# Spreading the sample group's decays through DRAM, and taking the output gates one tile early, in a fused RWKV-7 / HGRN2 step

## The chip, the cores and the metric

The kernel runs on one core of a Trainium2 chip. The core has a matrix engine (TensorE, "PE" in the profile, with its weight loads as "PEld"), three elementwise engines (VectorE "DVE", ScalarE "ACT", GpSimd "POOL"), a sequencer that issues transfers (SyncE "SP"), and 16 DMA engines that carry them. Each engine works through its own instructions in the order of the program and waits on semaphores where an instruction needs another engine's result. The metric is the device time of one execution in microseconds. The kernel before was run three times: 1065.17 us is the median, 1065.13 and 1065.8 the ends.

## What is computed

One inference step of a decoder layer for two groups of rows: 256 prompt tokens of one new sequence, and 8 sequences ("samples") with 8 new tokens each. Both are 320 columns of the same products. Cut to what matters here:

```python
h = rms_norm(x, norm_g)
p = h @ w_in                      # one projection, 2048 x 12416
# branch A: RWKV-7, 16 heads of 64
decay = exp(-exp(w_log))
for t in tokens:                  # per sample and head, from the state s handed in
    sa = s @ kk[t]
    s  = s * decay[t] - outer(sa, kk[t] * a[t]) + outer(v[t], k[t])
    y[t] = s @ r[t]
y_a = (group_norm(y) + bonus) * silu(p_za)
# branch B: HGRN2 linear recurrence, times its own gate -> y_b
merged = sigmoid(p_ga) * (y_a @ proj_a) + sigmoid(p_gb) * (y_b @ proj_b)
y = x + merged @ w_out            # then a final rms_norm
```

Returned are the two groups' outputs and the new states. The change concerns two places: the factor by which a sample's old RWKV state `s` is multiplied over its 8 tokens (one number for each sample, head and key), and the gates `sigmoid(p_ga)` and `sigmoid(p_gb)`.

## The kernel before

**Precision by parts.** A float32 weight tile of 1024 x 128 is fetched (`raw`, 512 KB), cast by ACT to a rounded part `whi`, and DVE forms the rest `wlo = raw - whi`. Each product is then three matmuls: `whi` with the high part of the data, `whi` with its low part, `wlo` with its high part. Three buffers of each of `raw`, `whi` and `wlo` turn in a ring; one block of 8 x 3 = 24 matmuls over 320 columns uses one of them.

**Four stages.** A start (norm, transposes, the first blocks); a recorded stage, in which the projection runs beside both recurrences; the gate stage (the loop at L1622); and the output product with the final norm.

**The recorded stage.** `record_all` (L1530) records every operation of every engine, the class `Recorder` (L79) then lists them in the order of a planned schedule: it walks through time with a cost for each operation and a latency for each dependency, and picks by longest remaining path. All of it is emitted at L199, so rows of the profile there are told apart by tile names. The projection's matmuls write the tile `mps`, small products write `bank` (six PSUM banks, lent in turn). DMAs are issued on SP in the planned order. A DMA that goes through a DRAM scratch tile is planned with 4500 ns from issue to data.

**A head pair.** `rwkv(p, ...)` (L916) handles two heads of 64, for p = 0 to 7 ("first" to "eighth pair"). Rows of a tile are 2 heads x 64 keys or values. `B` is the running sum of the log decays, and `f` (L955) holds their exponentials: columns 0 to 7 for the prompt's four chunks, columns 8 to 15 the whole decay of each of the 8 samples, with the key on the partition. The old sample states `s0` have the head and value on the partition, and sample and key along the row, so `f` has to be turned and repeated over 64 values. `samples()` does that by products (L1211 to L1227): POOL copies `f` into `fh` and `fq`, DVE forms the low parts in `fq`, POOL multiplies `fq` by an identity pattern to get `fd` (128 x 256, twice), PE multiplies `fd` by a block of ones (`jr_sum`) into a bank, and DVE multiplies `s0` by that bank. Later DVE adds the new outer products (tile `big`, PE output) to `s0`, and SP stores it.

A different round trip through DRAM, in every pair: `nd` (buffer name `big`) and `dns` go to scratch tiles `scr` and `scrs`, and come back into `ww` as small triangular blocks that DVE inverts step by step (rows `big<-ww`, `ww<-ww,big`). All such transfers and the weight fetches share SP's queue.

**The gate stage.** For each of 16 tiles m of 128 output columns: the gate `ga` is fetched from DRAM where it was made in the recorded stage (m < 7) or made here (48 matmuls into `mps`, then three ACT operations in `sigm`), the gate `gbt` is made here, then 24 matmuls into `ppa` (`y_a` by `proj_a`), 24 into `ppb`, and DVE and ACT merge them. Ahead of the loop `split` (L1611) divides `ya` and `yb` into high and low parts `yah`, `yal`, `ybh`, `ybl`: four ACT casts and four DVE subtractions each.

Of the kernel before, what the change touches and what calls it, by code (L numbers as in the profile page):

```python
# [9 lines left out]
F32 = mybir.dt.float32  # L10
F32R = mybir.dt.float32r
# [8 lines left out]
NT = NP_ + NS  # L20
NSEQ = 8
LS = 8
KT = D // 128
# [404 lines left out]
def hybrid_step(ctx, tc, x_prompt, x_sample, state_rwkv, state_hgrn, state_shift, norm_g, w_in,  # L428
# [4 lines left out]
    V, S, G, T = nc.vector, nc.scalar, nc.gpsimd, nc.tensor  # L433

    S.add_instruction(mybir.InstLoadActFuncSet(
        name=nc.get_next_instruction_name(), act_func_set_id=EXP_LN_SET, ins=[], outs=[]))
# [30 lines left out]
    HS = [slice(0, 64), slice(64, 128)]  # L467
# [29 lines left out]
    def run(gen):  # L497
        for _ in gen:
            pass
# [3 lines left out]
    def main(c0, post, pre=()):  # L503
        ps = psm.tile([128, 512], F32, name="mps", tag="m")
        yield from project(ps[:, :NT], win, c0, KT, hhi, hlo, pre)
        post(ps[:, :NT])


    with tc.tile_pool(name="start", bufs=1) as st, \
# [63 lines left out]
        id32 = ctile([128, 32], "id32")  # L573
# [245 lines left out]
    def sigm(out, in_, bias=0.0, sign=1.0):  # L819

        S.activation(out, in_, AF.Exp, scale=-sign, bias=bias)
        S.activation(out, out, AF.Ln, bias=1.0)
        S.activation(out, out, AF.Exp, scale=-1.0)
# [36 lines left out]
             "w1": 384, "w2": 320, "w3": 320, "ks": 128, "rhs2": 128, "ye": 192, "ket": 256, "o": NT}  # L860


    CLEAR = {"uB", "uE", "ys", "dn", "rhs", "rhs2", "k3", "vm", "w1", "vt", "att", "attc", "az", "rz"}

    def at(name, shape=(128, NT), tag=None, bufs=1, dt=F32):
        tag = tag or name
        return ring(pa, tag, list(shape), bufs, dt, SIZES.get(tag), tag in CLEAR)

# [4 lines left out]
    def aps(name="aps"):  # L873
        book.loans += 1
        at_ = lent[0]
        return bass.AP(at_.tensor, at_.offset + book.loans * LOAN, [list(d_) for d_ in at_.ap])
# [39 lines left out]
    def rwkv(p, r, k, v, za):  # L916
# [9 lines left out]
        s0 = at("s0", (128, NSEQ, 64))  # L926
# [10 lines left out]
        s = at("s", tag="uS")  # L937
# [4 lines left out]
        a = at("a", tag="uA")  # L942
# [9 lines left out]
        B = at("B", tag="uB")  # L952
        V.tensor_tensor_scan(B, rs_a, s, 0.0, op0=ALU.mult, op1=ALU.add)
        e = at("e", (128, 16))
        f = at("f", (128, 16), bufs=2)  # L955
        V.tensor_copy(e[:, 0:4], B[:, 31:NP_:64])
        Bp = B[:, :NP_].rearrange("p (c t) -> p c t", t=64)
        V.tensor_sub(Bp, Bp, e[:, 0:4, None].to_broadcast([128, 4, 64]))
# [7 lines left out]
        S.activation(e2, B, AF.Exp, scale=C0)  # L966
        S.activation(f[:, 0:4], e[:, 0:4], AF.Exp, scale=C0)
        S.activation(f[:, 4:16], e[:, 4:16], AF.Exp, scale=-C0)

        uv = at("uv", (128, 5, 2, 64))  # L970
        G.memset(uv[0:64, 0:5:2], 0.0)
# [48 lines left out]
        az = at("az", (128, 2, 2, 96))  # L1020
# [50 lines left out]
        for i in range(1, 7):  # L1071
            m = 7 - i
# [128 lines left out]
        def samples():  # L1201
            rhs = at("rhs2", (128, 64))
            S.copy(rhs, psr[:, :64])
            yield
            pu = aps("pu2")
            T.matmul(pu[:, :64], ys.rearrange("p h t -> p (h t)"), rhs, start=True, stop=True)
            for h in range(2):
                S.copy(uv[0:64, 4, h], pu[HS[h], 0:64])


            fh = at("fh", (128, 8), dt=F32R)  # L1211
            fq = at("fq", (128, 2, 8), dt=F32R)
            G.tensor_copy(fh, f[:, 8:16])
            for h in range(2):
                for hf in range(2):
                    src, dst = (slice(64 * h + 32 * j, 64 * h + 32 * j + 32) for j in (hf, 0))
                    G.tensor_copy(fq[dst, hf], f[src, 8:16])
                    dst = slice(64 * h + 32, 64 * h + 64)
                    V.tensor_sub(fq[dst, hf], f[src, 8:16], fh[src].bitcast(F32))
            pf = aps("pf")  # L1220
            for hf in range(2):
                fd = at("fd", (128, NSEQ, 32), dt=F32R)
                G.tensor_mul(fd, id32[:, None, :].to_broadcast([128, NSEQ, 32]),
                             fq[:, hf, :, None].bitcast(F32).to_broadcast([128, NSEQ, 32]))
                T.matmul(pf[:, 256 * hf:256 * hf + 256], jr_sum, fd.rearrange("p s k -> p (s k)"), start=True, stop=True)
            V.tensor_mul(s0.rearrange("p s (a k) -> p a s k", a=2), s0.rearrange("p s (a k) -> p a s k", a=2),
                         pf.rearrange("p (a s k) -> p a s k", a=2, s=NSEQ))  # L1227
            yield

            uh = at("uh", (128, 128), tag="rhs2")  # L1230
            for a_ in range(2):
                S.copy(uh[64 * a_ + 32:64 * a_ + 64], uv[64 + 32 * a_:96 + 32 * a_, 4].rearrange("p h v -> p (h v)"))
            for a_ in range(2):
                S.copy(uh[64 * a_:64 * a_ + 32], uv[32 * a_:32 * a_ + 32, 4].rearrange("p h v -> p (h v)"))
            bm = at("bm", (128, 4, 128), tag="big")
            for si in range(4):
                S.activation(bm[:, si], bk[:, 4], AF.Copy, scale=seq4[:, si:si + 1])
            pds = [aps("pd2") for _ in HS]
            side_by_side([((pds[a_][HS[h], :256], uh[HS[a_], 64 * h:64 * h + 64], bm[HS[a_], :, 64 * h:64 * h + 64]),
                           dict(start=True, stop=True)) for h in range(2) for a_ in range(2)])  # L1240
            for a_ in range(2):
                s0h = s0[:, 4 * a_:4 * a_ + 4]
                V.tensor_add(s0h, s0h, pds[a_][:, :256].rearrange("p (s k) -> p s k", s=4))
            Y.dma_start(s_rwkv[0, :, 2 * p:2 * p + 2].rearrange("s h v k -> (h v) s k"), s0)
            yield
# [243 lines left out]
    prompt_ = [scr.tile([512, 32], F32, name=f"scr{j}", tag=f"scr{j}") for j in range(2)]  # L1489
    turned = scr.tile([960, 128], F32, name="scrt", tag="scrt")  # L1490
    turned_i = scr.tile([NT, 128], F32, name="scri", tag="scri")
    pieces = lambda t_: t_.rearrange("(b x) (q c) -> q x b c", x=32, q=4)
    quads = [slice(32 * q_, 32 * q_ + 32) for q_ in range(4)]
    sample_ = [scr.tile([128, 8], F32, name=f"scrs{j}", tag=f"scrs{j}") for j in range(2)]
# [124 lines left out]

    yah, yal = split(ya, "ya", fpr, "yah")  # L1620
    ybh, ybl = split(yb, "yb", ypool, "ya")
    for m in range(KT):  # L1622
        ga = fpr.tile([128, NT], F32, name="ga", tag="ga", bufs=2)
        if m < NLATE:
            nc.sync.dma_start(ga, late[m])
        else:
            run(main(OFF_GA + 128 * m, lambda ps: sigm(ga, ps)))
        gbt = fpr.tile([128, NT], F32, name="gbt", tag="gbt", bufs=2)
        run(main(OFF_GB + 128 * m, lambda ps: sigm(gbt, ps)))
        ps = psf.tile([128, 512], F32, name="ppa", tag="f")  # L1630
        run(project(ps[:, :NT], proj_a[0], 128 * m, 8, yah, yal))
        mt = fpr.tile([128, NT], F32, name="mt", tag="mt", bufs=2)
        V.tensor_mul(mt, ga, ps[:, :NT])
        ps = psf.tile([128, 512], F32, name="ppb", tag="f")
        run(project(ps[:, :NT], proj_b[0], 128 * m, 8, ybh, ybl))
        V.tensor_mul(gbt, gbt, ps[:, :NT])
        V.tensor_add(mt, mt, gbt)
        S.copy(mhi[:, m, :], mt[:, :NP_])
        V.tensor_sub(mlo[:, m, :], mt[:, :NP_], mhi[:, m, :].bitcast(F32))
        S.copy(ms[:, m, 0], mt[:, NP_:])  # L1640
        V.tensor_sub(ms[:, m, 1], mt[:, NP_:], ms[:, m, 0].bitcast(F32))
# [168 lines left out]
```

## Time and profile before

| | before |
|---|---|
| median of 3 runs | 1065.17 us |
| the profiled execution's own time | 1065.99 us |
| its span, first to last instruction | 1063.8 us |
| granted TensorE clock, mean | 0.997 |
| DMA engines, mean rate | 168 GB/s |

The profiled execution is 0.82 us above the median, and 2.2 us of its time lie outside the span. Busy times of the engines overlap. A matmul's own duration (some 310 ns for 320 columns) also overlaps that of its neighbours; what a matmul costs PE is the step from its start to the next start, which is 0.147 us between two matmuls of 320 columns. A number in square brackets behind a row is the idle time of that engine just before it, and what ended it.

### The profile page before, as it was taken

To read this page: it belongs to the slowest core of one execution; us is meant where nothing else is said; L and a number is where in the kernel's file an instruction comes from. 1 tells how busy PE (TensorE), PEld (TensorE's weight loads), DVE (VectorE), ACT (ScalarE), POOL (GpSimd) and SP (SyncE) were. 2 spreads that over 40 slices of the span, in tenths; PEclk is the share of its full clock that TensorE was granted. 3 is DMA by queue.
4 is the path that set the end of the run, shared out by engine and by line. 5 is a ranking of instruction groups with operands and counts; after the bars stand their busy time and mean duration, and the time that the engine had idled before them with its cause. 6 is when DMAs were issued, how large, how long until landed. Compare 5 with 4: busy or idle time off the path is not lost.

```text
span 1063.8 us, 23012 instructions
## 1 busy us (share of the span) xinstructions
PE 1045.8 (98%) x8740; PEld 1010.4 (95%) x8740; DVE 763.5 (72%) x1616; ACT 697.9 (66%) x1608; POOL 127.8 (12%) x361
## 2 busy tenths in 40 slices
PE   7999999999999999999999999999999999999996
PEld 6999999999999999999999999999999999988885
DVE  8789989999999898998988857444444444446532
ACT  7757878978879689788687787444444444445412
POOL 9511201212112013112011000000000000000000
PEclk9999999999999999999999999999999999999998
DMA  6776585684865856849757647555555555497402
GB/s 202 198 184 163 126 228 142 162 224 121 216 165 123 223 147 171 210 115 214 184 139 194 175 115 219 170 165 148 156 145 152 152 146 155 144 296 266 152 17 99
DMA packets 356370, 178.78 MB, mean 168 GB/s; under 512 B 82013, under 2 KB 345440, under 8 KB 355684
## 3 DMA queue, kind: packets, MB, share of 16 engines
q1 hardware_dynamic: 355892, 176.01, 60.4%
q8 instruction: 68, 1.11, 0.4%
q10 hardware_dynamic: 368, 1.31, 0.3%
q14 instruction: 42, 0.34, 0.1%
HBM read 159.97 MB, written 17.32 MB: 167 GB/s over the span
## 4 chain that ended last, share of the span: by engine, by line
PE 94%; POOL 2%; ACT 1%; DVE 1%; DMA 1%; issue 0%; DVEq 0%; ACTq 0%; POOLq 0%
PE mps L199 47%; PE bank L199 10%; PE mps L494 5%; PE mps L493 5%; PE mps L492 5%; PE po L1682 3%; PE po L1681 3%; PE po L1683 3%; PE ppb L493 2%; PE ppb L494 2%; PE ppb L492 2%; PE ppa L494 2%; PE ppa L493 2%; PE ppa L492 2%; PE po L1687 1%; PE po L1686 1%
## 5 line engine op out<-in xcount | busy, mean ns | idle before, releaser
L199 PE MATMUL mps<-hhi,whi 128*128 128x320 f32 x1136 | 356.7, 314 | 0.0
L199 PE MATMUL mps<-hlo,whi 128*128 128x320 f32 x1136 | 355.7, 313 | 0.0
L199 PE MATMUL mps<-hhi,wlo 128*128 128x320 f32 x1136 | 354.7, 312 | 0.0
L199 PEld LDWEIGHTS mps<-hhi,whi 128*128 128x128 f32 x1136 | 213.6, 188 | 3.2 <-issue 2.3
L199 PEld LDWEIGHTS mps<-hlo,whi 128*128 128x128 f32 x1136 | 213.7, 188 | 1.2 <-issue 0.4
L199 PEld LDWEIGHTS mps<-hhi,wlo 128*128 128x128 f32 x1136 | 213.6, 188 | 1.1 <-issue 0.4
L199 DVE TENSOR_TENSOR wlo<-raw,whi 128x1024 fp32r<-128x1024 f32 x140 | 171.4, 1224 | 23.2 <-ACT whi L199 21.7
L482 ACT CAST whi<-raw 128x1024 fp32r<-128x1024 f32 x82 | 86.0, 1048 | 148.5 <-PE mps L493 93.7
L483 DVE TENSOR_TENSOR wlo<-raw,whi 128x1024 fp32r<-128x1024 f32 x82 | 100.4, 1225 | 113.3 <-ACT whi L482 113.1
L199 ACT CAST whi<-raw 128x1024 fp32r<-128x1024 f32 x140 | 146.2, 1044 | 44.0 <-PE mps L199 34.1
L493 PE MATMUL mps<-hlo,whi 128*128 128x320 f32 x400 | 123.6, 309 | 0.0
L494 PE MATMUL mps<-hhi,wlo 128*128 128x320 f32 x400 | 123.6, 309 | 0.0
L492 PE MATMUL mps<-hhi,whi 128*128 128x320 f32 x400 | 123.6, 309 | 0.0
L492 PEld LDWEIGHTS mps<-hhi,whi 128*128 128x128 f32 x400 | 75.1, 188 | 0.0
L493 PEld LDWEIGHTS mps<-hlo,whi 128*128 128x128 f32 x400 | 75.1, 188 | 0.0
L494 PEld LDWEIGHTS mps<-hhi,wlo 128*128 128x128 f32 x400 | 75.1, 188 | 0.0
L1670 DVE TENSOR_TENSOR wlo<-raw,whi 128x1024 fp32r<-128x1024 f32 x32 | 38.6, 1222 | 36.7 <-ACT whi L1669 36.5
L1669 ACT CAST whi<-raw 128x1024 fp32r<-128x1024 f32 x32 | 33.1, 1051 | 47.6 <-PE po L1686 21.7
L1681 PE MATMUL po<-whi,mhi 128*128 128x512 f32 x128 | 50.0, 391 | 0.0
L1683 PE MATMUL po<-wlo,mhi 128*128 128x512 f32 x128 | 50.0, 391 | 0.0
L1682 PE MATMUL po<-whi,mlo 128*128 128x512 f32 x128 | 50.0, 391 | 0.0
L493 PE MATMUL ppb<-ybl,whi 128*128 128x320 f32 x128 | 39.7, 310 | 0.4 <-DVE ybl L1617 0.4
(415 smaller groups left out, 1986.3 us busy)
## 6 DMA issues: line engine op xcount, KB each, us to landing
raw<-in_w_in_dram SPq DMA_DIRECT2D x194, 512.0 KB
raw<-in_w_out_dram SPq DMA_DIRECT2D x32, 512.0 KB
raw<-in_proj_a_dram SPq DMA_DIRECT2D x16, 512.0 KB
raw<-in_proj_b_dram SPq DMA_DIRECT2D x16, 512.0 KB
s<-in_state_hgrn_dram SPq DMA_DIRECT2D x8, 512.0 KB
ww<-scr SPq DMA_DIRECT2D x8, 512.0 KB
out_dram<-s SPq DMA_DIRECT2D x8, 512.0 KB
scrt<-ww SPq DMA_DIRECT2D x32, 120.0 KB
```

The costliest lines, as they stand in the source:

```text
L199: o.fn(*(real(x) for x in o.args), **{k: real(x) for k, x in o.kw.items()})
L482: S.copy(hi[:, ks], raw[:, ks])
L483: sub.tensor_sub(lo[:, ks], raw[:, ks], hi[:, ks].bitcast(F32))
L492: T.matmul(dst, hi[:, q, :], xhi[:, k, :], start=(k == 0), stop=False)
L493: T.matmul(dst, hi[:, q, :], xlo[:, k, :], start=False, stop=False)
L494: T.matmul(dst, lo[:, q, :], xhi[:, k, :], start=False, stop=(k == nk - 1))
L1669: S.copy(hi, raw)
L1670: V.tensor_sub(lo, raw, hi.bitcast(F32))
L1681: T.matmul(pt, h, hi, start=first, stop=False)
L1682: T.matmul(pt, l, hi, start=False, stop=False)
L1683: T.matmul(pt, h, lo, start=False, stop=end)
L1686: T.matmul(pt, h, hi, start=first, stop=False)
```

## The change

Two edits.

**The decays.** `f` becomes 32 columns wide and is cleared once. Right after `f` is written, DVE transposes it in blocks of 32 x 32 into `ft`. Four DMAs on SP write the sample rows of `ft` to a DRAM tile `decays` (named `scrf` in the profile), as [2 heads x 8 samples, 64 keys], and two DMAs read it back into a tile `spread`, each repeating 512 numbers over 64 partitions. The products are gone: `fh`, `fq`, `fd` and the bank. DVE multiplies `s0` by `spread`.

**The gates.** What makes `ga` and `gbt` of tile m becomes a function, and the loop calls it for tile m + 1 ahead of tile m's products with `proj_a` and `proj_b`, with three buffers of each gate for two.

```diff
-    CLEAR = {"uB", "uE", "ys", "dn", "rhs", ...}
+    CLEAR = {"uB", "uE", "ys", "dn", "f", "rhs", ...}
@@ rwkv
-        f = at("f", (128, 16), bufs=2)
+        f = at("f", (128, 32), bufs=2)
...
+        ft = at("ft", (128, 32))
+        V.transpose(ft, f)
+        for q_ in range(4):
+            Y.dma_start(decays[8 * (q_ // 2):8 * (q_ // 2) + 8, 32 * (q_ % 2):32 * (q_ % 2) + 32], ft[32 * q_ + 8:32 * q_ + 16])
+        spread = at("spread", (128, NSEQ, 64))
+        for h in range(2):
+            Y.dma_start(spread[HS[h]].rearrange("p s k -> p (s k)"),
+                        decays[8 * h:8 * h + 8].rearrange("s k -> (s k)")[None].to_broadcast([64, 512]))
@@ samples
-            fh = at("fh", (128, 8), dt=F32R)
-            fq = at("fq", (128, 2, 8), dt=F32R)
-            G.tensor_copy(fh, f[:, 8:16])
-            for h in range(2):
-                for hf in range(2):
-                    src, dst = (slice(64 * h + 32 * j, 64 * h + 32 * j + 32) for j in (hf, 0))
-                    G.tensor_copy(fq[dst, hf], f[src, 8:16])
-                    dst = slice(64 * h + 32, 64 * h + 64)
-                    V.tensor_sub(fq[dst, hf], f[src, 8:16], fh[src].bitcast(F32))
-            pf = aps("pf")
-            for hf in range(2):
-                fd = at("fd", (128, NSEQ, 32), dt=F32R)
-                G.tensor_mul(fd, id32[:, None, :].to_broadcast([128, NSEQ, 32]),
-                             fq[:, hf, :, None].bitcast(F32).to_broadcast([128, NSEQ, 32]))
-                T.matmul(pf[:, 256 * hf:256 * hf + 256], jr_sum, fd.rearrange("p s k -> p (s k)"), start=True, stop=True)
-            V.tensor_mul(s0.rearrange("p s (a k) -> p a s k", a=2), s0.rearrange("p s (a k) -> p a s k", a=2),
-                         pf.rearrange("p (a s k) -> p a s k", a=2, s=NSEQ))
+            V.tensor_mul(s0, s0, spread)
@@ gate stage
-    for m in range(KT):
-        ga = fpr.tile([128, NT], F32, name="ga", tag="ga", bufs=2)
+    def gates(m):
+        ga = fpr.tile([128, NT], F32, name="ga", tag="ga", bufs=3)
         if m < NLATE:
             nc.sync.dma_start(ga, late[m])
         else:
             run(main(OFF_GA + 128 * m, lambda ps: sigm(ga, ps)))
-        gbt = fpr.tile([128, NT], F32, name="gbt", tag="gbt", bufs=2)
+        gbt = fpr.tile([128, NT], F32, name="gbt", tag="gbt", bufs=3)
         run(main(OFF_GB + 128 * m, lambda ps: sigm(gbt, ps)))
+        return ga, gbt
+
+    made = [gates(0)]
+    for m in range(KT):
+        if m + 1 < KT:
+            made.append(gates(m + 1))
+        ga, gbt = made[m]
         ps = psf.tile([128, 512], F32, name="ppa", tag="f")
```

The schedule of the recorded stage is planned anew from these operations, so its order shifts on every engine. The first place is SP in the third pair, where the samples' decays now leave and come back beside the round trip of the triangular blocks. Before:

```order
L199 DMA out_dram<-ks_544 128x128
L199 DMA raw<-in_w_in_dram 128x8x128
L199 DMA scr_476<-big_526 32x4x32 x4
L199 DMA scrs_480<-dns_527 64x2x8
L199 DMA uv_518<-scrt 64x3x128
L199 DMA uv_518<-scrt 64x2x128
L199 DMA raw<-in_w_in_dram 128x8x128
L199 DMA w2a_0_506<-in_rwkv_a_dram 64x128
L199 DMA ww<-scr_476 128x1x1024
L199 DMA ww<-scrs_480 16x8x8
```

And with the change:

```order
L199 DMA scrf<-ft_519 8x32 x4
L199 DMA raw<-in_w_in_dram 128x8x128
L199 DMA scr_476<-big_529 32x4x32 x4
L199 DMA scrs_481<-dns_530 64x2x8
L199 DMA s_0_510<-in_state_rwkv_dram 128x8x64
L199 DMA uv_521<-scrt 64x3x128
L199 DMA uv_521<-scrt 64x2x128
L199 DMA spread_520<-scrf 64x512 x2
L199 DMA raw<-in_w_in_dram 128x8x128
L199 DMA out_dram<-s_0_535 128x8x128
L199 DMA ww<-scr_476 128x1x1024
L199 DMA ww<-scrs_481 16x8x8
```

The two reads into `spread` stand ahead of one weight fetch and of the read into `ww`. The second place is DVE in the same pair, where the inversion begins (`big<-ww`). Before (`q` and `yb` are of branch B, `ya` is branch A's result):

```order
L199 TENSOR_TENSOR fq_550<-f_515,fh_549 32x8
L199 SCALAR_TENSOR_TENSOR o_541<-o_541,cols,w_0_535 128x320
L199 TENSOR_TENSOR q_500<-q_500,w_0_533 128x320
L199 TENSOR_TENSOR yb<-o_541,w_0_539 128x320
L199 TENSOR_TENSOR wlo<-raw,whi 128x1024
L199 TENSOR_TENSOR ya<-bk_522,sg_557 128x320
L199 TENSOR_TENSOR big_526<-ww 128x30
```

And with the change:

```order
L199 TENSOR_TENSOR wlo<-raw,whi 128x1024
L199 SCALAR_TENSOR_TENSOR o_544<-o_544,cols,w_0_538 128x320
L199 TENSOR_TENSOR q_501<-q_501,w_0_536 128x320
L199 TENSOR_TENSOR yb<-o_544,w_0_542 128x320
L199 TENSOR_TENSOR ya<-bk_525,sg_558 128x320
L199 TENSOR_TENSOR rl_513<-bon_524,rh_512 128x320
L199 TENSOR_TENSOR s_0_510<-s_0_510,spread_520 128x512
L199 TENSOR_TENSOR wlo<-raw,whi 128x1024
L199 TENSOR_TENSOR big_529<-ww 128x30
```

The small `fq` row is gone, and the product of `s0` (here `s_0`) with `spread` stands just ahead of a split of weights (`wlo<-raw,whi`) and of the inversion. The third place is DVE where the gate stage begins. Before:

```order
L483 TENSOR_TENSOR wlo<-raw,whi 128x1024 x3
L1617 TENSOR_TENSOR yal<-ya,yah 128x640 x4
L483 TENSOR_TENSOR wlo<-raw,whi 128x1024
L1617 TENSOR_TENSOR ybl<-yb,ybh 128x640 x4
L1633 TENSOR_TENSOR mt<-ga,ppa 128x320
```

And with the change:

```order
L483 TENSOR_TENSOR wlo<-raw,whi 128x1024 x4
L1611 TENSOR_TENSOR yal<-ya,yah 128x640 x4
L483 TENSOR_TENSOR wlo<-raw,whi 128x1024
L1611 TENSOR_TENSOR ybl<-yb,ybh 128x640 x4
L483 TENSOR_TENSOR wlo<-raw,whi 128x1024 x2
L1634 TENSOR_TENSOR mt<-ga,ppa 128x320
```

The four splits ahead of `yal` now belong to the gates of tiles 0 and 1 (before: the gate of tile 0, then `proj_a` and `proj_b`). On PE 96 matmuls of the two gates stand ahead of the first `ppa` row, where 48 stood before, and behind that row the order is 24 into `ppa`, 24 into `ppb`, then the gate matmuls of the tile after next.

More of the change, by code (lines that the diff above doesn't have):

```diff
@@ L860, in hybrid_step @@
              "w1": 384, "w2": 320, "w3": 320, "ks": 128, "rhs2": 128, "ye": 192, "ket": 256, "o": NT}
-    CLEAR = {"uB", "uE", "ys", "dn", "rhs", "rhs2", "k3", "vm", "w1", "vt", "att", "attc", "az", "rz"}
+    CLEAR = {"uB", "uE", "ys", "dn", "f", "rhs", "rhs2", "k3", "vm", "w1", "vt", "att", "attc", "az", "rz"}
     def at(name, shape=(128, NT), tag=None, bufs=1, dt=F32):
@@ L1491, in hybrid_step @@
     turned_i = scr.tile([NT, 128], F32, name="scri", tag="scri")
+    decays = scr.tile([16, 64], F32, name="scrf", tag="scrf")
     pieces = lambda t_: t_.rearrange("(b x) (q c) -> q x b c", x=32, q=4)
```

## The prediction

> **What bounds the kernel now.** The page comes first: busy times with their shares of the span, and the chain that ended last by engine.
>
> ```profile
> PE 1045.8 (98%) x8740; PEld 1010.4 (95%) x8740; DVE 763.5 (72%) x1616; ACT 697.9 (66%) x1608; POOL 127.8 (12%) x361
> PE 94%; POOL 2%; ACT 1%; DVE 1%; DMA 1%; issue 0%; DVEq 0%; ACTq 0%; POOLq 0%
> ```
>
> PE is busy for 98% of the span and is 94% of the chain, so a change is worth what it takes off PE's instructions and what it takes out of PE's idle time. The second view, the windows by stage (stretch, length, then PE, PEld, DVE, ACT and POOL busy with counts, clock, DMA share, GB/s), says where that idle time is.
>
> ```profile
> 38.00:640.00 602.00, 600.17 (x5973) 587.62 (x5972) 534.14 (x1298) 485.75 (x1270) 96.68 (x283) 1.00 0.66 170
> 640.00:670.00 30.00, 29.30 (x199) 28.77 (x197) 19.76 (x25) 20.22 (x36) 0.00 (x0) 1.00 0.76 218
> 670.00:1045.00 375.00, 375.00 (x2299) 356.14 (x2298) 173.12 (x210) 158.19 (x232) 0.00 (x0) 1.00 0.53 161
> ```
>
> The recorded stage has 1.8 us of idle PE, the passage into the gate stage 0.7 us, the rest of the gate stage and the output product none; what stands before and behind these windows is not touched. So the second edit can gain only at the passage, and the first only its products and at most those 1.8 us with what hangs on them. The third view, PE's waits (total, times, longest), names the owners:
>
> ```profile
> PE bank L199 <- POOL fd L199: 1.5, 3, 0.6
> PE ppb L493 <- DVE ybl L1617: 0.4, 1, 0.4
> PE ppa L493 <- DVE yal L1617: 0.3, 1, 0.3
> ```
>
> Most of the idle time belongs to `fd`, which goes, and to the split of `ya` and `yb`, which gets more time. All three lines are things that the change is aimed at.
>
> **The change part by part: the products.** The group of `fd` products (durations shortest/median/longest, first and last start) and one of them in order of time:
>
> ```profile
> L199 PE MATMUL bank<-fd,jr_sum x16: 277/278/387, 66.6 to 578.7; 128*128 128x256 f32 x16
> 140.26 0.28 PE L199 MATMUL bank<-fd,jr_sum 128*128 128x256 f32 x1
> 140.38 0.30 PE L199 MATMUL mps<-hhi,whi 128*128 128x320 f32 x1
> ```
>
> A product costs PE the step to the next start, 140.38 - 140.26 = 0.12 us. Sixteen of them: **-1.9 us**. Three of the sixteen also came late:
>
> ```profile
> 349.82 0.31 PE L199 MATMUL mps<-hhi,wlo 128*128 128x320 f32 x1
> 350.56 0.38 PE L199 MATMUL bank<-fd,jr_sum 128*128 128x256 f32 x1 [0.43 <-POOL fd L199]
> 350.79 0.31 PE L199 MATMUL mps<-hhi,whi 128*128 128x320 f32 x1
> ...
> 426.50 0.31 PE L199 MATMUL mps<-hhi,wlo 128*128 128x320 f32 x1
> 427.21 0.39 PE L199 MATMUL bank<-fd,jr_sum 128*128 128x256 f32 x1 [0.40 <-POOL fd L199]
> ...
> 575.89 0.31 PE L199 MATMUL mps<-hlo,whi 128*128 128x320 f32 x1
> 576.83 0.39 PE L199 MATMUL bank<-fd,jr_sum 128*128 128x256 f32 x1 [0.64 <-POOL fd L199]
> ```
>
> The steps into them are 0.74, 0.71 and 0.94 us in place of 0.15, so 0.59 + 0.56 + 0.79 = 1.94; the step out of the first is 0.23 for 0.12, and with 0.11 for each the stalls are worth **-2.3 us**. What is late next there? Of the 1.83 us of idle PE in the recorded stage `fd` owns 1.5, which leaves 0.3 for all other causes: no second one stands right behind it.
>
> **The passage.** PE's rows where the first `ppa` and the first `ppb` products wait for the split:
>
> ```profile
> 654.98 0.31 PE L492 MATMUL ppa<-yah,whi 128*128 128x320 f32 x1
> 655.63 0.41 PE L493 MATMUL ppa<-yal,whi 128*128 128x320 f32 x1 [0.34 <-DVE yal L1617]
> 655.89 0.30 PE L494 MATMUL ppa<-yah,wlo 128*128 128x320 f32 x1
> ...
> 659.25 0.31 PE L492 MATMUL mps<-hhi,whi 128*128 128x320 f32 x1
> 659.92 0.41 PE L493 MATMUL ppb<-ybl,whi 128*128 128x320 f32 x1 [0.36 <-DVE ybl L1617]
> 660.18 0.31 PE L494 MATMUL ppb<-ybh,wlo 128*128 128x320 f32 x1
> ```
>
> Steps of 0.65, 0.26, 0.67 and 0.26 us for 0.15 each: 1.24 us. The change puts the 48 matmuls of the second gate, 48 x 0.147 = 7 us, ahead of the first `ppa` row, and the order on DVE leaves four weight splits ahead of `yal` as before. The lateness of 0.5 us is covered many times over: **-1.2 us**. Past the passage PE is 375.00 of 375.00 busy and its instructions are the same, only moved: nothing.
>
> **What is added to PE's order.** Counted from the order, the number of matmuls drops by just the 16. Two things shift. The products of `big`, in 64 x 64 tiles of the array, stand alone between 128 x 128 products in all eight pairs; before, two of the eight stood behind another tiled group and shared its switch. The small full-array product `bank<-st,arp` follows an `mps` product 18 times, before 23.
>
> ```profile
> 254.40 0.31 PE L199 MATMUL mps<-hhi,wlo 128*128 128x320 f32 x1
> 254.64 0.66 PE L199 MATMUL bank<-big,rhs 64*64 64x256 f32 x8
> 255.23 0.42 PE L199 MATMUL mps<-hhi,whi 128*128 128x320 f32 x1
> 255.49 0.22 PE L199 MATMUL bank<-st,arp 128*128 128x64 f32 x1
> ```
>
> The step into `big` is 0.24 for 0.15, and the group that stood ahead of it now has an exit of its own, for which I allow as much again: two times 0.2, **+0.4 us** (bounds 0.2 and 0.7). The step from `mps` to `st,arp` is 0.26 for 0.15; five fewer are 0.55 us, of which I take half, since the small product now has another neighbour to pay for: **-0.3 us** (bounds -0.6 and 0).
>
> **What is added beside PE.** DVE, by its groups (mean ns behind the busy time):
>
> ```profile
> L199 DVE TENSOR_TENSOR fq<-f,fh 32x8 fp32r<-32x8 f32 x32 | 5.1, 160 | 0.9
> L199 DVE STREAM_TRANSPOSE ww<-bk 128x640 f32<-128x640 f32 x8 | 6.7, 838 | 0.1
> L199 DVE STREAM_TRANSPOSE ww<-v 128x320 f32<-128x320 f32 x8 | 4.0, 500 | 0.2
> L199 DVE TENSOR_TENSOR s<-s,bank 128x512 f32<-128x512 f32 x24 | 16.4, 685 | 0.8 <-PE bank L199 0.3
> L1732 DVE TENSOR_TENSOR xa<-xa,xb 128x512 f32<-128x512 f32 x6 | 4.0, 684 | 1.3 <-ACT jk L1702 1.3
> ```
>
> 32 rows of `fq` leave (5.1 us). A transpose of 32 columns is some 0.5 - 288 x 0.338/320 = 0.2 us, eight of them 1.6 us. Multiplying `s0` costs 685 ns with a bank and should cost as much with `spread` (684 ns with both inputs in SBUF). DVE gets 3.5 us lighter over 600, and POOL, 12% busy, loses its copies and `fd`; neither bounds, so nothing is counted for it. The four clears of `f` on POOL run in its idle time.
>
> SP gets 48 DMAs, six in each pair. What matters is not their issue but two new waits: the reads into `spread` wait on SP for the writes to land, with a weight fetch, a store and the read into `ww` queued behind; and DVE's `s0` by `spread` waits for the reads, with `wlo` splits behind, for which PE waits. The nearest rows are the other round trip:
>
> ```profile
> 495.36 0.63 SPq L199 DMA_DIRECT2D ww<-scrs  x1
> 502.97 0.19 DVE L199 TENSOR_TENSOR big<-ww 128x30 f32<-128x30 f32 x1 [3.74 <-DMA ww<-scrs]
> 495.00:515.00 20.00, 20.00 (x140) 19.96 (x140) 15.34 (x38) 11.50 (x21) 1.73 (x4) 1.00 0.92 231
> SPq L199 <- DMA scrs<-ww: 7.5, 7, 1.7
> ```
>
> That read took 7.6 us from issue to data, DVE stood for 3.74 us, and PE was busy for 20.00 of the 20.00 us around it. On SP the existing pair of write and read made it wait for 1.7 us at most, and PE for nothing. In four pairs (first, third, seventh, eighth) the order leaves the time of two weight blocks, 2 x 24 x 0.147 = 7.1 us, between the earliest issue of `spread` and its use; in the other four far more. So DVE should wait for up to a microsecond or so in four pairs, well inside the 3.74 us that cost nothing. Bounds: 0; and four stalls as long as the `fd` ones, 4 x 0.7 = 2.8. Near the covered row I take **+0.4 us**.
>
> [...]
>
> **The sum.** -1.9 - 2.3 - 1.2 + 0.4 - 0.3 + 0.4 = -4.9 us. Against the profiled execution's own 1065.99 us that is 1061.1; this execution lies 0.82 us above the median of the runs, so the median should be 1065.17 - 4.9 = **1060.3 us**.
>
> **The rivals.**
>
> *The waits come back as DMA waits.* The same order that put `spread` ahead of `ww` delays the inversion, where DVE already stood for 3.74 us, and PE loses 0.4 to 0.7 us in most pairs, as it did three times to `fd`, 3.5 us or more in all. For it: DMA share 0.92 there, and 256 KB more for each pair. Against it: 20.00 of 20.00. It gives 1063 to 1067, say 1064: the forecast without its +0.4, and 3.5 to 4 on top.
>
> *Slower: SP as a new bound.* If landing of the small writes takes so long under load that each of eight reads holds SP while the ring of three `raw` buffers runs empty, PE stalls in every pair. It decides where the hold outlasts the cover: the gain of 4.9 is used up at 0.6 us of open stall in each pair, and it is slower by over 0.2% at 0.9 us in each: 1068. The seven holds seen, 1.7 us at most and uncounted on PE, speak against it.
>
> *The passage doesn't do what it says.* The fetch of `ga` and the casts `yah` wait for memory of the recorded stage to come free, and the split could slip with them; then 1.2 us stay: 1061.5.
>
> *More than the sum.* If the new order also puts more small products side by side: 1058.5.
>
> **How the numbers follow.** The forecast (1059 to 1062.5) has 0.60, the passage 0.10, the DMA waits 0.17, slower 0.07, more 0.06. A measurement of this kernel can tell about 0.2%, 2.1 us, from no change: faster is below 1063.0, slower above 1067.3. Faster then has 0.60 + 0.10 + 0.06 = 0.76, the same 0.17, slower 0.07. The range goes from the forecast's lower end, which is that of all unknown costs at their low ends (-1.9 - 2.3 - 1.2 + 0.2 - 0.6 + 0 = -5.8, 1059.4) and a little of the case of more, to 1064.8, which takes in their high ends (-5.4 + 0.7 + 0 + 2.8 = -1.9, 1063.3) and two thirds of the DMA waits; about 0.17 lies outside.
>
> **What would show it.** After: no PE wait on POOL; no PE wait on `yal` or `ybl`; PE idle in the recorded stage under 1 us; steps of 0.15 us throughout the passage. DVE's product with `spread` waiting for a DMA in the first, third, seventh or eighth pair, with PE busy beside it, would bear the cover out. Wrong would be: PE idle behind `wlo` or `whi` rows, ACT's casts waiting for `raw` more than now, or a stall of a new owner in the recorded stage.

## The result: slower, and the profile after

| | before | after |
|---|---|---|
| median, five runs each | 1065.17 us | 1072.0 us (1070.01 to 1074.87) |
| ratio to before, 95% interval | | 1.0066 [1.0055, 1.0076] |
| profiled execution: time, span | 1065.99, 1063.8 us | 1074.87, 1073.1 us |

The profiled execution of the changed kernel is the slowest of its five, 2.9 us above the median; what follows reads where its time lies, and the experiments go by medians and ratios. First its page (busy times with shares and counts, then the chain by engine).

```profile
PE 1046.4 (98%) x8724; PEld 1008.8 (94%) x8724; DVE 753.6 (70%) x1592; ACT 699.1 (65%) x1608; POOL 107.1 (10%) x309
PE 86%; DVE 6%; DMA 4%; ACT 2%; issue 1%; SPq 0%; DVEq 0%; ACTq 0%
```

PE's busy time has hardly moved, but it is 86% of the chain where it was 94%: DVE and DMAs have come in. The windows by stage (columns as in the prediction):

```profile
38.00:640.00 602.00, 589.64 (x5881) 574.60 (x5880) 517.66 (x1264) 478.81 (x1255) 75.39 (x227) 1.00 0.66 170
640.00:680.00 40.00, 40.00 (x275) 39.95 (x274) 25.01 (x30) 28.72 (x52) 0.00 (x0) 1.00 0.72 208
680.00:1050.00 370.00, 370.00 (x2275) 351.90 (x2275) 174.53 (x214) 157.32 (x231) 0.00 (x0) 1.00 0.53 160
```

The passage and all behind it are full. The recorded stage has 12.4 us of idle PE where it had 1.8. PE's waits in that stage (total, times, longest) name new owners, and none of the three of before:

```profile
PE bank L199 <- DVE es L199: 3.6, 3, 1.9
PE mps L199 <- DVE wlo L199: 3.2, 4, 1.2
PE bank L199 <- issue: 2.9, 3, 2.0
PE mps L199 <- ACT whi L199: 1.4, 1, 1.4
PE bank L199 <- ACT yz L199: 1.1, 1, 1.1
```

From start to start, PE's rows give the account. The sixteen steps into `fd` products were 4.3 us and are gone; the steps at the passage are 1.2 us shorter; and twelve steps of the recorded stage are too long by 0.57 to 2.18 us, 14.3 us in all. -5.5 + 14.3 is 8.8 of the 9.3 us by which the spans differ. So the gain came and something else took it back. Behind PE's stalls stand ACT and DVE, and behind them DMAs. The longest waits of these two on DMAs in the same stage:

```profile
ACT big L199 <- DMA bk<-scrt: 12.8, 4, 6.9
ACT whi L199 <- DMA raw<-in_w_in_dram: 10.9, 9, 2.7
DVE big L199 <- DMA ww<-scrs: 8.6, 3, 4.0
DVE big L199 <- DMA ww<-scr: 7.8, 2, 4.5
DVE wlo L199 <- DMA scrs<-ww: 3.8, 1, 3.8
```

The two rows `DVE big` are the start of the inversion. The row `DVE wlo` is of the sixth pair: there the cast `whi` that `wlo` needs came late, behind ACT's 6.9 us for `bk`. Before, the same rows were these, with none for `wlo`:

```profile
DVE big L199 <- DMA ww<-scrs: 6.7, 4, 3.7
ACT whi L199 <- DMA raw<-in_w_in_dram: 6.5, 4, 2.5
DVE big L199 <- DMA ww<-scr: 0.8, 1, 0.8
ACT big L199 <- DMA bk<-scrt: 0.7, 2, 0.4
```

DVE now waits 16.4 us for `ww` where it waited 7.5. The product with `spread`, for which the prediction expected waits, has none on a DMA: its eight rows show 0.3 us of idle time ahead of them, on PE. What is late in three pairs is what stands behind the new transfers: the two reads are issued between the write and the read of the triangular blocks in the third and eighth pair, the four writes in the sixth, and DVE waits there for 3.15, 4.01 and 4.48 us. In the first and fourth pair, with 3.35 and 1.48 us, no new transfer stands in that stretch. SP's timeline in the sixth pair (start, duration of the issue, transfer):

```profile
421.14 2.02 SPq L199 DMA_DIRECT2D scr<-big  x4
423.26 0.59 SPq L199 DMA_DIRECT2D scrs<-dns  x1
423.89 0.60 SPq L199 DMA_DIRECT2D s<-in_state_rwkv_dram  x1
424.59 0.54 SPq L199 DMA_DIRECT2D out_dram<-s  x1
425.23 2.34 SPq L199 DMA_DIRECT2D scrf<-ft  x4
427.67 1.01 SPq L199 DMA_DIRECT2D raw<-in_w_in_dram  x1
428.77 0.53 SPq L199 DMA_DIRECT2D w2a<-in_rwkv_a_dram  x1
429.36 0.59 SPq L199 DMA_DIRECT2D ww<-scr  x1
```

Rows stand end to end: SP itself is busy, most transfers taking it 0.5 to 0.6 us. The four small writes take 2.34 us of SP between the write of the triangular blocks and the read that brings them back. And they need not stand there: ACT wrote `f` at 379.89 us, and DVE transposed it at 422.06.

```profile
379.89 0.20 ACT L199 ACTIVATE f<-e 128x12 f32<-128x12 f32 x1
422.06 0.20 DVE L199 STREAM_TRANSPOSE ft<-f 128x32 f32<-128x32 f32 x1
```

The planner picks by longest remaining path; the decays have much slack, and their transpose is put last, 42 us late. In the third, fifth and eighth pair it is 35, 41 and 21 us late.

### The profile page after: what moved, and what is told of

Same layout as the page of the kernel before. It is cut to its first block, busy times and chain, and to the rows that moved or that the text cites. A ratio compares the mean times of both kernels' runs of the same rounds, so it can differ in the third digit from the quotient of the medians.

```text
span 1073.1 us, 22947 instructions
## 1 busy us (share of the span) xinstructions
PE 1046.4 (98%) x8724; PEld 1008.8 (94%) x8724; DVE 753.6 (70%) x1592; ACT 699.1 (65%) x1608; POOL 107.1 (10%) x309
## 4 chain that ended last, share of the span: by engine, by line
PE 86%; DVE 6%; DMA 4%; ACT 2%; issue 1%; SPq 0%; DVEq 0%; ACTq 0%
PE mps L199 37%; PE bank L199 10%; PE mps L492 5%; PE mps L494 5%; PE mps L493 5%; PE po L1684 3%; PE po L1682 3%; PE po L1683 3%; DVE wlo L199 2%; PE ppb L492 2%; PE ppa L492 2%; PE ppb L494 2%; PE ppa L494 2%; PE ppa L493 2%; PE ppb L493 2%; PE po L1688 1%
## 5 line engine op out<-in xcount | busy, mean ns | idle before, releaser
L492 PE MATMUL ppa<-yah,whi 128*128 128x320 f32 x128 | 39.6, 309 | 0.0
```

The lines of the kernel that those rows point to most:

```text
L492: T.matmul(dst, hi[:, q, :], xhi[:, k, :], start=(k == 0), stop=False)
```

## The experiments

Two theories stood at first. A: the six transfers of each pair do the harm, by their place on SP (A1) or by what they take from the DMA engines (A2). B: the new planned order does it, whatever the transfers do. All ratios are to runs of the kernel before on the same chip, with 95% intervals; 0.001 is 1.07 us.

**1. Each edit alone, the transfers away, the transfers on another queue.** `gates_alone` and `decays_alone` take one hunk of the change each.

> The kernel before with the second edit alone (gates one tile early, three buffers of each). If the passage was worth what the prediction said, 1.2 us, it gives 1063.9 to 1064.2 us, and no PE wait on yal or ybl is left. If the loss of the whole change lay in this edit, it would be 1071 or more; the trace of the changed kernel, with 40.00 of 40.00 us of PE busy there, speaks against that.

Measured: 1064.13 us, **0.9985 [0.9976, 0.9995]**; 40.00 of 40.00 us of PE at the passage.

> The changed kernel with the loop of before in the gate stage, so the first edit alone. If the two edits don't touch each other it is the changed kernel plus 1.2 us, 1072 to 1074 us, with the passage's two waits on yal and ybl back.

Measured: 1075.0 us, **1.0083 [1.0063, 1.0103]**. The second edit is worth its 1.2 us (here 1.6, and 1.8 as the difference to the changed kernel); the loss lies in the first.

```diff
         for o in book.order():
+            if any(u[0].startswith("scrf") for u in o.uses):
+                if "scrf" not in o.args[0].tensor.name:     # no_dmas
+                    nc.gpsimd.memset(o.args[0], 1.0)
+                # pool_queue: nc.gpsimd.dma_start(*o.args, **o.kw)
+                continue
             book.emit(o)
```

> The changed kernel in its own planned order, with the six transfers of each pair left out where they stood (the four writes into the DRAM tile and the two reads back; spread is filled with ones on POOL instead, so the sample states are not decayed). Theory A, the transfers do it (their places in SP's queue or the traffic): PE's idle time in the recorded stage falls from 12.4 us to under 3, time 1059 to 1062. Theory B, the new planned order does it whatever the transfers do: 1068 to 1072, idle 9 us or more.

Measured: 1066.66 us, **1.0009 [0.9999, 1.0018]**; 3.4 us of idle PE. Between the theories: the transfers cost 0.0057, some 6 us; but 1.0009 is far above the 0.995 that the removed work should give. The order takes some 6 us too. DVE's waits for `ww` are 9.3 us in all here, so 7 of the 16.4 us come with the transfers. The order's cost is not in the sum of these waits: `old_order` below has 9.6 us of them.

> The changed kernel in its own planned order, with the six transfers of each pair issued by POOL at their places instead of by SP. Theory A1, what hurts is that the reads wait on SP for the writes to land with weight fetches and the ww read queued behind them: 1059 to 1063. Theory A2, what hurts is what the transfers take from the 16 DMA engines: 1068 to 1073, as with SP. Theory B, the order: 1068 to 1073 too.

Measured: 1070.46 us, **1.0042 [1.0027, 1.0057]**. Less than half of the transfers' cost goes when POOL issues them, so this run alone doesn't choose between A1 and A2. In its trace the time from the first write to the read's issue is 7.4 us on the mean, as in `no_dmas` (7.3), and yet PE is idle for 6.9 us in place of 3.4. In the sixth pair the read takes 8.8 us from issue to use where `no_dmas` has 6.3, which speaks for A2 there; two further stalls, 2.9 us together, have no releaser in the profile. What is left of the transfers' cost on POOL stays open.

**2. The order of before, kept.** In `old_order` the recorded program and its plan are those of before; the products are skipped as it is emitted. `early` adds the transpose and the transfers by hand; `dense` moves them.

```diff
+        for p_ in range(8):      # planned times, ns
+            t0 = max(at_[fop[p_]], at_[times[p_ - 1]] if p_ else 0)
+            events += [(t0 + 1000, 0, p_), (t0 + 2000, 1, p_), (t0 + 11000, 2, p_)]   # transpose, writes, reads
         for o in ready:
+            while events and at_[o.n] >= events[0][0]:
+                decay(*events.pop(0)[1:])
+            if o.n in out_ops:   # fh, fq, fd and the bank
+                continue
```

> The planned order of before, kept op by op, with the products left out as it is emitted (fh, fq, fd, the matmuls into the bank) and s0 multiplied by a constant tile of ones, so the sample states are not decayed; the gates' edit is in, no transfer is added. It prices the removal alone. By the prediction's terms -1.9 -2.3 -1.2 = -5.4 us against before, so about 1060 us, with PE idle under 0.5 us in the recorded stage. If instead another stall waits right behind those on fd (the removal is worth little), 1063 or more.

Measured: 1060.49 us, **0.9944 [0.9929, 0.9959]**, 1.2 us of idle PE in the stage. The removal is worth what the prediction's terms said, and a little more (6.0 us for 5.4).

> The same order of before without the products, and the whole of the new way of the decays (transpose, four writes, two reads, product with spread), with the six transfers put by hand on SP ahead of the stretch of the triangular blocks, the reads 9 us of planned time behind the writes. Theory place (the transfers hurt where they stand among the round trips): 1060 to 1062, as without them. Theory traffic (they hurt by what they take from the DMA engines and SP wherever they stand): 1063 to 1066. Theory order (the new plan does most of it): 1060 to 1062.

Measured: 1060.95 us, **0.9942 [0.9926, 0.9959]**. This is the whole change, computing everything, at the time of the kernel without any transfer: 0.0124 under the changed kernel, some 13 us, and faster than the kernel before.

> As early, but from the second pair on the four writes stand right behind the write of dns into scrs, and the two reads right ahead of the read into ww. Theory place: the waits of DVE's first inversion step for ww grow by 2 to 4 us in most pairs, PE gets stalls on wlo, whi or es, 1064 to 1069. Theory order: under 1062, since this order leaves more work beside the wait. Theory traffic: as early.

Measured: 1076.41 us, **1.0095 [1.0076, 1.0114]**. The same operations on every engine in the same order, but for six transfers and a transpose in seven of the eight pairs: 15 us. The windows of the recorded stage, `early` first:

```profile
38.00:640.00 602.00, 599.96 (x5961) 586.60 (x5960) 525.71 (x1274) 485.82 (x1271) 67.00 (x229) 1.00 0.68 174
```

```profile
38.00:640.00 602.00, 591.18 (x5785) 575.91 (x5784) 517.05 (x1258) 474.32 (x1243) 69.06 (x230) 1.00 0.68 171
```

The DMA share is 0.68 in both; 2.0 us of idle PE against 10.8. SP's rows and the inversion's first row, in the sixth pair, of `early`:

```profile
418.40 1.74 SPq L199 DMA_DIRECT2D scr<-big  x4
420.25 0.61 SPq L199 DMA_DIRECT2D scrs<-dns  x1
...
424.41 0.59 SPq L199 DMA_DIRECT2D ww<-scrs  x1
...
432.44 0.19 DVE L199 TENSOR_TENSOR big<-ww 128x30 f32<-128x30 f32 x1 [1.71 <-DMA ww<-scr]
```

And of `dense`:

```profile
427.80 1.74 SPq L199 DMA_DIRECT2D scr<-big  x4
429.63 0.62 SPq L199 DMA_DIRECT2D scrs<-dns  x1
430.30 1.50 SPq L1623 DMA_DIRECT2D scrf<-ft  x4
...
433.85 2.44 SPq L1627 DMA_DIRECT2D spread<-scrf  x2
...
436.98 0.59 SPq L199 DMA_DIRECT2D ww<-scrs  x1
...
443.38 0.19 DVE L199 TENSOR_TENSOR big<-ww 128x30 f32<-128x30 f32 x1 [3.26 <-DMA ww<-scr]
```

From the first write to the last read's issue it is 6.0 us in the one, 9.2 in the other; from that issue to DVE's start 8.0 and 6.4. Once issued, the read is no later for the traffic ahead of it; it is issued later. Not all of that is bare issue: the two reads into `spread` hold SP for 2.44 us, and such a read takes 0.554 us at the median of the changed kernel's sixteen. Over the eight pairs these holds are some 4 us, and the wait for the writes that the prediction named can be in them.

PE does not stand while DVE waits in the sixth pair. Its stalls in `dense` come later, on another product:

```profile
PE bank L199 <- DVE rl L199: 7.2, 5, 1.9
```

`rl` is a DVE result of the same pair, 13 to 18 us behind the first row of the inversion, and in between DVE has no gap of more than 0.6 us. So a wait for `ww` is passed on whole, and PE's five stalls on `rl` (0.99 to 1.87 us) stand 14 to 19 us behind waits of 2.98 to 5.67 us.

> The changed kernel with nothing new but the planner's latencies: 7000 ns in place of 4500 for a transfer through a DRAM scratch tile, 9000 in place of 6500 for the wide read into ww. If the loss comes from a plan that takes these round trips for shorter than they are, it gives 1059 to 1064 and PE idle under 5 us in the recorded stage; if any new plan of these operations is as bad, or the transfers hurt whatever is planned, 1068 or more.

Measured: 1089.92 us, **1.0216 [1.02, 1.0231]**. The miss is large: longer latencies make DVE wait less for `ww` (1.4 us in all), but the plan stretches the loop (the wide read into `ww` was planned with 6500 ns, the other transfers through scratch tiles with 4500), and PE stands up to 5.5 us at a time for results from ACT. The planner's latency was no plain error.

**3. Which transfers, and which half of the changed kernel's loss.**

> As dense (1.0095 of before), but the transpose and the four writes early; only the two reads stand right ahead of the read into ww, with nothing to wait for. Theory traffic in front (256 KB ahead of the wide read): most of the loss stays, 1070 or more. Theory SP (each transfer holds SP for some 0.6 us and the reads wait for the writes): two of six are left and no wait, so 1063 to 1067.

Measured: 1066.75 us, **0.9997 [0.9985, 1.0008]**.

> As dense, but the two reads right behind the reads into ww; only the four small writes stand ahead. Theory traffic in front: nearly all of the loss goes, 1060 to 1063. Theory SP: four of six are left, 1064 to 1070. If both halves cost less than half of dense's 15 us, the cover of DVE is a threshold.

Measured: 1075.29 us, **1.0078 [1.0061, 1.0094]**. The four writes of 1 KB cost 14 us, the two reads of 128 KB 6 us, all six 15: that fits the number of transfers on SP, though not in proportion, and not their bytes. (In `dense_writes` the reads still follow, ahead of `bk` and of weight fetches, and in the third pair they stand ahead of the read into `ww`, so a part of the 14 may be theirs.) A2 falls as the main cause in this order. The round trip's times, worked out from SP's and DVE's rows (means of the eight pairs, from the first `scr<-big` issue to the issue of `ww<-scrs`, and from there to the first `big<-ww`), with DVE's wait there summed:

| | write to read issued | issued to used | DVE's wait, sum | ratio |
|---|---|---|---|---|
| before | 7.4 us | 6.3 us | 7.5 us | 1 |
| `early` | 7.6 | 6.3 | 11.4 | 0.9942 |
| `dense_reads` | 8.8 | 6.1 | 18.7 | 0.9997 |
| `dense_writes` | 9.1 | 6.2 | 21.0 | 1.0078 |
| `dense` | 10.0 | 6.0 | 26.3 | 1.0095 |

(In `early` the reads of the eighth pair still stand inside the stretch.) The second column hardly moves. The first grows with the loss, though not in proportion: against `early` it is in eight pairs 9.2, 11.7 and 18.6 us more in `dense_reads`, `dense_writes` and `dense`, for 6, 14 and 15 us of time. Weight fetches behind the same transfers are late too: ACT's casts wait for `raw` for 17.7 us in `early` and 26.5, 29.4 and 32.2 us in the three. No run separates their share; PE's waits name `rl` first in all three (4.5, 6.2 and 7.2 us), and never `whi`.

> The changed kernel in its own planned order, all of the computation kept, but the transpose and the six transfers of each pair moved by hand to the place that early gives them: writes 2 us of planned time behind f (or behind the product of the pair before), reads 9 us later. Theory place: the transfers' share of the loss goes and the plan's stays, so the time of no_dmas, 1065 to 1068. If the plan's loss goes too (it came from the transpose and waits), 1062 or less; if the place doesn't matter in this order, 1070 or more.

Its edit emits the changed kernel's own plan with the same `events`. Measured: 1068.27 us, **1.0017 [1.0005, 1.0029]**. The place is worth 0.0049, 5 us, in this order too; the rest stays with the plan.

> Neither the transpose nor the transfers are recorded, so the planner doesn't see them either; s0 is multiplied by a constant tile of ones, so the sample states are not decayed; the rest as in the changed kernel, planned anew. If the worse plan comes from planning around the transfers, it is as old_order, 0.993 to 0.996 of before (1060 to 1062). If it comes from the removal alone (any new plan can fall either way), it is as no_dmas, 0.999 to 1.002 (1065 to 1068).

Measured: 1061.22 us, **0.9945 [0.9931, 0.996]**. So the removal by itself doesn't spoil the plan.

**4. What spoils the plan.** Theories left: the transfers' low urgency, the SP and DVE time booked for them, or chance. The edits of the planner (`jitter_a` has `MARGIN` 410 for 400, `jitter_b`, `after_b` and `ranked_b` have `SPARE` 22 for 20):

```diff
+            if any(u[0].startswith(("ft", "scrf")) for u in o.uses):
+                o.rank += 1e6     # ranked;   unbooked has o.cost = 1
```

> The changed kernel with one rule added to the planner: the transpose into ft and the six transfers get the highest urgency, so each runs as soon as f is there, some 30 to 45 us ahead of the triangular blocks, and the rest is planned around them. If what spoils the plan is only that low urgency puts them last, into the round trips, it gives 1060 to 1063. If a plan that has to fit six more transfers is worse wherever they stand, 1065 to 1069, as after_early (1.0017 of before).

Measured: 1072.64 us, **1.0054 [1.0038, 1.007]**. In the profiled execution (1067.99 us, the fastest of the seven) each transpose runs within 2 us of `f`, and DVE waits 2.9 us in all for `ww`, less than before; but PE waits 4.9 us in small tiled products for which the profile names no releaser. Low urgency explains the place, not the plan.

> The changed kernel planned with a cost of 1 ns for the transpose and the six transfers, urgency unchanged. If the planner's booking of SP's and DVE's time for them spoils the plan, the rest of the plan comes out as in plan_without: 1061 to 1064, or a little more where the real transfers then collide. If it is the product's new dependency that moves the plan, 1066 or more.

Measured: 1061.56 us, **0.995 [0.9934, 0.9967]**. The whole change, computing everything, with one rule in the planner: as fast as `early`. In this plan the transpose stands 0.7 to 6 us behind `f`, and the transfers ahead of the round trips, without having been told to. So low urgency alone does not put them last; in the changed kernel it did so together with the time booked for them.

> plan_without (0.9945 of before) with one planner constant moved by a hair: 410 ns in place of 400 of margin for small products on PE. It leaves out the decay of the sample states, as plan_without. If the loss of the plan is a thing of chance (any plan can come out some us better or worse), this one differs from plan_without by 2 us or more; if plans of the same operations come out alike, it is 1060 to 1062.5.

Measured: 1065.39 us, **0.9986 [0.9977, 0.9996]**, 4.2 us above `plan_without`.

> As jitter_a, with another constant moved: 22 ns in place of 20 of spare time behind each operation of DVE, ACT and POOL. Chance: 2 us or more from plan_without, either way; no chance: 1060 to 1062.5.

Measured: 1061.71 us, **0.9953 [0.9938, 0.9968]**. A small step in a planner constant can cost 4 us, or nothing.

> The changed kernel, nothing left out, with the planner's constant of jitter_b (22 ns of spare time in place of 20). In its order the writes still stand between scrs and ww in the third, sixth and eighth pair. If the loss hangs on that place, it stays at 1.003 or more of before; if the whole of it is chance in the plan, it can be anything from 0.995 to 1.007, and I would expect under 1.000.

Measured: 1065.41 us, **0.9992 [0.9982, 1.0002]**. The changed kernel itself, with 22 for 20: 7 us faster, and no slower than before, though the writes stand among the round trips in three pairs. There other transfers happen to stand elsewhere: from first write to read issued it is 6.2 us on the mean, and DVE waits 0.9 us for `ww` in all.

> ranked (transfers first, 1.0054 of before) with the same constant moved. If planning around booked transfers spoils a plan whatever it is, 1.003 to 1.008; if it was chance, under 1.000, like plan_without (0.9945) and unbooked (0.995).

Measured: 1076.71 us, **1.0097 [1.0082, 1.0112]**. This is slower than either theory had said, and 0.0043 from `ranked`.

Plans made without the transfers' cost: 0.9945, 0.995, 0.9953, 0.9986. Plans made with it: 0.9992, 1.0009 (transfers left out), 1.0054, 1.0066, 1.0097. `slow_plan` (1.0216) is of the second group too, with longer latencies besides. The two groups don't overlap, but four and five draws, whose members lie up to 4 and up to 11 us apart, are few, and they are not quite alike: of the first only `unbooked` runs the transfers, of the second all but `no_dmas`. That booking them makes plans worse is likely and not settled. That a plan of the same operations can move by 4 to 8 us for a step of 2.5 or 10% in one planner constant is shown.

## Why the prediction was wrong

**Right: the products and PE's stalls on `fd`** (-1.9 and -2.3), **and the passage** (-1.2). `old_order` has all three and gives 6.0 us for 5.4, its interval from 4.4 to 7.6; `gates_alone` gives 1.6 (0.5 to 2.6) for 1.2. No PE wait on POOL, `yal` or `ybl` is left, as foretold.

**Wrong: "What matters is not their issue but two new waits" (+0.4, bounds 0 to 2.8).** It is mostly their issue, and the term was 6 us (0.0057, against `no_dmas`), 5 of them by place (0.0049, against `after_early`); in `dense` the place costs 15 us against `early`. SP was taken for a queue with room; in the stretch between the write and the read of the triangular blocks it has none (its rows of the sixth pair stand end to end from 421.14 to 429.95 us), and each transfer put there delays the loop by its issue, at the median 0.295 us for a write into `scrf` and 0.554 us for a read into `spread`. Of the two waits that were priced, the product with `spread` waited for no DMA. Whether the reads' wait for the writes counts is open: in the sixth pair they hold SP for 3.61 us, with `bk` behind them, but in `no_dmas` SP stands as long at the same place, in the row of `bk` itself (3.10 us). The bound of 2.8 was taken from PE's stalls on `fd`, an unlike thing; the row that should have set it was SP's own timeline around the read into `ww`.

**Wrong: the cover.** "DVE stood for 3.74 us, and PE was busy for 20.00 of the 20.00 us" was true of the seventh pair. There, after the change, DVE doesn't wait at all. The waits came in the first, third, fourth, sixth and eighth pair (3.35, 3.15, 1.48, 4.48, 4.01 us), where ACT and DVE hold the splits of weights in the same order behind them, and nothing said that PE had 3.7 us in hand there. The window of 20 us was also too short to show the cover: it ends 12 us behind the wait, and the DVE result on which PE stands in `dense` comes 18 us behind it. Before, in the same seventh pair:

```profile
520.75 0.48 DVE L199 TENSOR_TENSOR rl<-bon,rh 128x320 fp32r<-128x320 f32 x1
522.04 0.31 PE L199 MATMUL bank<-rl,jr_sum 128*128 128x320 f32 x1
```

`rl` was done at 521.23 us, 0.81 us ahead of PE's product. That margin, 0.42 to 1.24 us in the second to eighth pair, is what a longer wait had in hand there.

**Wrong: the plan made anew as "+0.4 - 0.3".** The prediction counted how the new order changes PE's neighbours, and took its stalls to be those of the old order less the ones removed. A plan's stalls are drawn anew: in the changed kernel's order without any transfer PE stood 3.4 us in place of the 0.3 counted on, and the time was 6 us over that of `plan_without`. This half, some 8 us of the distance to `early` (1.0017 against 0.9942), had no term and no width in the range. No run prices the +0.4 and the -0.3 themselves.

**The rivals.** The first had the mechanism ("the same order that put `spread` ahead of `ww` delays the inversion") but too small a price, 0.4 to 0.7 us in most pairs and back to 1064; six stalls in the changed kernel are of 1.25 to 2.18 us. The second, SP as a new bound at 1068, had the right engine, for the wrong reason: mainly not a hold for the writes to land that runs the ring of `raw` empty, but the issue itself ahead of a read that closes a loop. The ring had some part: ACT waited for `raw` for 10.9 us where it had waited 6.5, and 3.7 in `no_dmas`.

The prediction's signs of being wrong all came: PE idle behind `wlo` and `whi` (4.6 us), more waiting of ACT's casts for `raw`, and stalls of new owners, `es` and `yz`.

## What to carry to other kernels

A queue's issue time is a resource: where a round trip through DRAM closes a loop, count the transfers that stand between its write and its read, not their bytes (here four writes of 1 KB cost 14 us and two reads of 128 KB 6 us), and put new ones with slack ahead of that stretch. A scheduler that goes by urgency can do the opposite, since it puts what has slack last. To see whether a wait is covered, go on from it to the next result on its engine that the bottleneck needs, and read by how much that result is early. And where a change makes a large plan anew, its forecast has a width of its own: time two or three plans of the same operations before the change is judged, or keep the old order by hand, which here gave 0.9942 for the change that measured 1.0066.

## What the runs showed of the hardware

In `no_dmas` a stall of PE cost more than its length. PE stood 1.90 us for `es`; then twelve steps between products of 320 columns are 0.267 us in place of 0.147, which is 1.4 us more. First PE's rows, then two windows:

```profile
448.86 0.31 PE L199 MATMUL mps<-hhi,wlo 128*128 128x320 f32 x1
451.07 0.33 PE L199 MATMUL bank<-ident,es 128*128 128x128 f32 x1 [1.90 <-DVE es L199]
...
452.00 0.47 PE L199 MATMUL mps<-hlo,whi 128*128 128x320 f32 x1
452.26 0.47 PE L199 MATMUL mps<-hhi,wlo 128*128 128x320 f32 x1
452.53 0.47 PE L199 MATMUL mps<-hhi,whi 128*128 128x320 f32 x1
```

```profile
452.00:455.00 3.00, 3.00 (x13) 3.00 (x13) 2.96 (x8) 2.36 (x6) 0.76 (x4) 0.50 0.94 270
455.00:458.00 3.00, 3.00 (x22) 3.00 (x21) 2.79 (x10) 2.73 (x11) 1.19 (x2) 1.00 0.78 217
```

PE counts as busy in both, with 13 products against 22; the granted clock, 0.50 and 1.00, tells them apart. The same stall of 1.90 us stands in four kernels of this plan. In `no_dmas` and `pool_queue` the clock was 0.50 behind it for some 3 us, in the changed kernel's profiled run it stayed at 1.00. Over the recorded stages of before, the changed kernel and the eight runs of the experiments 1 and 2, the clock fell behind stalls of 1.49 us (`decays_alone`, with 0.69 us of idle PE close behind it) to 5.5 us (`slow_plan`, where it fell before the stall's end), and not behind others of up to 2.9 us (`slow_plan`). So the length of a stall alone does not tell whether the clock falls behind it; what does, no run shows.
